# RWKV head pairs as two merged streams, with the dense products no longer tied behind their steps

## The chip, the cores and the metric

The kernel runs on one core of a Trainium2 chip. The metric is the device time of one execution in microseconds (us), the median of the runs shown.

## The reference

The reference is a block of two layers over 512 tokens of width 1024 in float32. Each layer is

```
x = x + 0.5 * swiglu(rms_norm(x, g_ffa), w_in_a, w_out_a)         # width 2816
h = rms_norm(x, g_mix);  z = h @ w_in                             # all branches' projections and the gates
ret  = retention(...)              # 8 heads, chunks of 128 tokens
dsa  = sparse_attention(...)       # 8 heads, top 128 keys by an index score
rwkv = rwkv7(...)                  # 8 heads of 64: token shift, low-rank decay, rate and gate, delta rule, group norm
x = x + sum over branches of sigmoid(gate_b) * (y_b @ p_b), through w_o
x = x + 0.5 * swiglu(rms_norm(x, g_ffb), w_in_b, w_out_b)
```

The RWKV part is a recurrence over the tokens: per head, a state of 64x64 is decayed, corrected by a rank-one term and read out at each token. The kernel computes it in chunks of 64 tokens. In a chunk the corrections depend on each other through a triangular matrix, which has to be inverted.

## The kernel before, in words

x is kept transposed (1024 features on 8 tiles of 128 partitions, 512 tokens). Every dense product runs in three passes on split operands (`mm3`, lines 109, 111, 113: high times high, high times low, low times high), so that one weight tile of 128 columns over 8 chunks is 24 products of 128x512. Weights come by DMA on SP's queue into four `raw` buffers (`load`, L54), are split by ScalarE and VectorE into three `whi` and three `wlo` buffers (`split`, L49 and L50), and each holds four chunks. TensorE writes to PSUM tiles `psd` (dense, 4 banks), `psr` (recurrence, 2) and `psf` (the rest, 2).

A mixer has three branches. `Ret` is retention by quarters, `Dsa` is the sparse attention, whose last part goes query tile by query tile and head pair by head pair: score products (`dot`, L710 and L711), a mask and softmax through VectorE, ScalarE and GpSimd (L805 to L810), turns of the weights L (L96), their split, and the products with v (L823, L824). Retention, attention, the 264-product gate blocks (`gates`) and the `merge` form one generator of dense work, `other()`. The third branch, `Rwkv`, goes by head pairs 0 to 3, and `pairs()` sets its order.

For a pair, `front` projects r, k and v (dense), `front2` makes decay, rate, the normalised key (turns of `bc`) and bonus, and the stacked operands `st` and `bk`. `mid` makes the chunk products z (L421, `psr<-stk,bk`), turns bk and v to token-major order, and inverts the triangles: their diagonal 32x32 blocks go to DRAM (`dn`) and back as `N`, one instance a partition (L457); GpSimd runs 31 steps on them (L466, L468); the inverse goes out as `dx` (L473) and back as `mt` (L479); 32 small products join the blocks (L487, L492). `chain` is the recurrence over 8 chunks, each of four dependent groups of products with copies by VectorE between (L504, L514, L524, L531, with the state `sv` made at L527). `post` is the group norm and the output: turns of Y (L96), scale and shift (L559), bonus (L561, GpSimd), gate product (L564) and its use (L565), then the result to DRAM, from where the merge reads it as `y` and splits it to `yh7` for pair 3.

The order of instructions on each engine is fixed when the kernel is built: a scheduler places instructions by the priority level in which they are traced ("rec" for the recurrence, then "split", "norm" for dense work, "late") with a simulated timeline, and an instruction may be tied behind another on its engine (`issue_after`). Before, the program ties dense work by hand. `K.fill(n, after)` (L78) traces n dense products of the queued work on TensorE behind a step of the pair, with counts from a table (lines 220 to 227):

```
FZ, FV, FD, FB, FE = 11, 38, 29, 5, 46
FP = 12, 11, 11, 15
FM = 6, 0, 2, 7
FC = 9, 7, 3, 5
```

An "urgent" queue gives the next pair's projections first place in it. Inside the inverse, after every fourth step, a pace product (L470, one column) waits for GpSimd's step, with dense products tied behind it, so that TensorE doesn't run ahead; there are 64 of them in the program. `pairs()` does, for each pair, the chain, then `next(p + 1)` (the next pair's `front2` and `mid`, tied behind the turns of v), then the `post`.

Of the kernel before, what the change touches and what calls it, by code (L numbers as in the profile page):

```python
# [7 lines left out]
P = 128  # L8
# [13 lines left out]
class Core:  # L22
    def __init__(self, tc, ctx):
        self.tc, self.nc, self.ctx = tc, tc.nc, ctx
        self.n = 0
        self.work, self.urgent, self.between = iter(()), deque(), True
        self.early = deque()
# [19 lines left out]
    def split(self, x, hi, lo):  # L47
        """exact parts of float32 for the one-pass products: x = hi + lo."""
# [8 lines left out]
    def wslot(self, src, n):  # L57
        """n <= 512 weight columns a partition, split."""
# [8 lines left out]
    def at(self, level):  # L67
        """what is traced here takes its place in that level of the scheduler's order."""
# [4 lines left out]
    def fill(self, n=None, after=None):  # L73
        """trace n products of the queued work, on the tensor engine behind `after`; n None: all that is urgent."""
        with ExitStack() as es:
            es.enter_context(self.at("norm"))
            if after:
                es.enter_context(self.tc.issue_after(after.ins))  # L78
            while n != 0 and (self.urgent or n):
                g = self.urgent[0] if self.urgent and self.between else self.work  # L80
                try:
                    new = next(g)
                except StopIteration:
                    if g is self.work:
                        break
                    self.urgent.popleft()
                    continue
                if g is self.work:
                    self.between = new
                if new == "wait":  # L90
                    break
                if n and not new:
                    n -= 1
# [11 lines left out]
    def mm3(self, out, a, b, start, stop):  # L105
        """three passes: hi*hi + hi*lo + lo*hi; a is stationary."""
# [9 lines left out]
    def dense(self, w, x):  # L116
        """w [128, K, 128] in DRAM, x: K split chunks of the transposed input -> PSUM [128 features, 512 tokens]."""
# [11 lines left out]
    def dense_tok(self, w, n, evac):  # L129
        """w [128, 8, n] in DRAM -> evac(token tile, PSUM [128 tokens, n features])."""  # L130
# [23 lines left out]
    def prep(self, x, c, gi, p):  # L154
        """chunk c of x^T -> split x*g, and its squares into the running sum."""
# [942 lines left out]
```

## Time and profile before

| | |
|---|---|
| median of 3 runs | 3111.48 us (3107.99 to 3112.62) |
| span of the profiled execution | 3103.6 us |
| around the span, against the median | 7.9 us |
| busy: TensorE, its weight loads | 2990.3 us, 2373.5 us |
| busy: VectorE, ScalarE, GpSimd | 1761.8, 1081.5, 715.2 us |
| products on TensorE | 14336 records |

The profiled execution is one of its own, not one of the three timed ones; the profile gives its span, and the table sets that against the median. TensorE is the bound, so the page is read by the time in which it is idle or runs at a lower clock: the windows give both by stretch, the list of waits tells for whom it waits, and the chain tells what lies behind the longest of these. A busy time counts a product's whole length although products are pipelined, so the spacing of starts, and not the mean length, tells what a product costs.

### The profile page before, as it was taken

To read this page: it belongs to the slowest core of one execution; us is meant where nothing else is said; L and a number is where in the kernel's file an instruction comes from. 1 tells how busy PE (TensorE), PEld (TensorE's weight loads), DVE (VectorE), ACT (ScalarE), POOL (GpSimd) and SP (SyncE) were. 2 spreads that over 40 slices of the span, in tenths; PEclk is the share of its full clock that TensorE was granted. 3 is DMA by queue.
4 is the path that set the end of the run, shared out by engine and by line. 5 is a ranking of instruction groups with operands and counts; after the bars stand their busy time and mean duration, and the time that the engine had idled before them with its cause. 6 is when DMAs were issued, how large, how long until landed. Compare 5 with 4: busy or idle time off the path is not lost.

```text
span 3103.6 us, 40717 instructions
## 1 busy us (share of the span) xinstructions
PE 2990.3 (96%) x14336; PEld 2373.5 (76%) x14336; DVE 1761.8 (57%) x3641; ACT 1081.5 (35%) x1892; POOL 715.2 (23%) x1186
## 2 busy tenths in 40 slices
PE   9999999999899999999999999999999899999998
PEld 7888877767667778888888888677776677788886
DVE  5443388758675675443344433887585746644433
ACT  4333343334333233333333333433333333333322
POOL 2110024342433031111011101243423340311100
PEclk9999999999899999999999999899999999999999
DMA  4223422223223452233322234222333135523232
GB/s 136 98 97 106 117 72 70 73 85 124 81 85 96 139 190 95 95 99 94 97 95 97 98 109 118 66 72 71 96 110 92 64 110 155 175 92 99 96 95 89
DMA packets 203580, 314.08 MB, mean 101 GB/s; under 512 B 46320, under 2 KB 60400, under 8 KB 203376
## 3 DMA queue, kind: packets, MB, share of 16 engines
q1 hardware_dynamic: 203376, 311.49, 32.2%
q8 instruction: 112, 1.84, 0.2%
q14 instruction: 92, 0.75, 0.1%
HBM read 277.86 MB, written 33.55 MB: 100 GB/s over the span
## 4 chain that ended last, share of the span: by engine, by line
PE 74%; DVE 10%; POOL 6%; DMA 6%; issue 3%; ACT 1%; SPq 0%; DVEq 0%; POOLq 0%; ACTq 0%
PE psd L113 22%; PE psd L109 22%; PE psd L111 22%; DMA N<-dn 3%; POOL cum L468 2%; POOL E L466 2%; DVE wlo L50 2%; PE psr L421 1%; DMA th<-th 1%; PE psr L504 1%; PE psf L96 1%; DMA dx<-cum 1%; DMA y<-y 1%; DVE cb L523 1%; PE psr L514 1%
## 5 line engine op out<-in xcount | busy, mean ns | idle before, releaser
L49 ACT ACTIVATE whi<-raw 128x512 fp32r<-128x512 f32 (+2 forms) x920 | 571.5, 622 | 1259.6 <-PE psd L111 927.2
L50 DVE TENSOR_TENSOR wlo<-raw,whi 128x512 fp32r<-128x512 f32 (+2 forms) x920 | 657.6, 715 | 560.0 <-ACT whi L49 543.9
L111 PE MATMUL psd<-xl,whi 128*128 128x512 f32 x2144 | 856.0, 399 | 2.4 <-DVE xl L161 2.4
L109 PE MATMUL psd<-xh,whi 128*128 128x512 f32 x2144 | 850.6, 397 | 1.5 <-DVE g L203 1.5
L113 PE MATMUL psd<-xh,wlo 128*128 128x512 f32 x2144 | 849.9, 396 | 0.1
L111 PEld LDWEIGHTS psd<-xl,whi 128*128 128x128 f32 x2144 | 406.7, 190 | 88.9 <-DVE xl L161 4.4
L109 PEld LDWEIGHTS psd<-xh,whi 128*128 128x128 f32 x2144 | 406.6, 190 | 88.5 <-issue 3.4
L113 PEld LDWEIGHTS psd<-xh,wlo 128*128 128x128 f32 x2144 | 406.9, 190 | 84.1 <-issue 1.4
L207 POOL TENSOR_TENSOR u<-s,u 128x512 f32<-128x512 f32 x88 | 141.2, 1605 | 841.0 <-DVE u L206 726.3
L109 PE MATMUL psd<-ah,whi 128*128 128x512 f32 x704 | 277.4, 394 | 0.0
L113 PE MATMUL psd<-ah,wlo 128*128 128x512 f32 x704 | 276.0, 392 | 0.0
L111 PE MATMUL psd<-al,whi 128*128 128x512 f32 x704 | 273.2, 388 | 0.0
L172 POOL TENSOR_TENSOR sq<-sq,sq 128x512 f32<-128x512 f32 x42 | 56.1, 1336 | 467.4 <-ACT sq L170 467.4
L113 PE MATMUL psd<-whi,xl 128*128 128x512 f32 (+1 forms) x384 | 160.6, 418 | 0.0
L111 PE MATMUL psd<-wlo,xh 128*128 128x512 f32 (+1 forms) x384 | 156.1, 407 | 0.0
L113 PEld LDWEIGHTS psd<-ah,wlo 128*128 128x128 f32 x704 | 132.1, 188 | 31.0
L109 PE MATMUL psd<-whi,xh 128*128 128x512 f32 (+1 forms) x384 | 155.1, 413 | 0.0
L111 PEld LDWEIGHTS psd<-al,whi 128*128 128x128 f32 x704 | 132.2, 188 | 29.6
L109 PEld LDWEIGHTS psd<-ah,whi 128*128 128x128 f32 x704 | 132.3, 188 | 26.3
L50 DVE TENSOR_TENSOR al<-u,ah 128x512 fp32r<-128x512 f32 x88 | 61.8, 702 | 153.6 <-ACT ah L49 153.4
L206 DVE TENSOR_TENSOR u<-psd,rb 128x512 f32<-128x512 f32 x88 | 60.9, 692 | 127.3 <-PE psd L113 127.3
L810 POOL TENSOR_SCALAR L<-L,mx 128x128 f32<-128x128 f32 (+3 forms) x64 | 71.4, 1118 | 199.4 <-DVE mx L809 99.0
(262 smaller groups left out, 3907.2 us busy)
## 6 DMA issues: line engine op xcount, KB each, us to landing
raw<-in_wf_dram SPq DMA_DIRECT2D x184, 256.0 KB
raw<-in_ffa_in_dram SPq DMA_DIRECT2D x176, 256.0 KB
raw<-in_ffb_in_dram SPq DMA_DIRECT2D x176, 256.0 KB
th<-th SPq DMA_DIRECT2D x96, 256.0 KB
raw<-in_ffa_out_dram SPq DMA_DIRECT2D x80, 256.0 KB
raw<-in_wt_dram SPq DMA_DIRECT2D x80, 256.0 KB
raw<-in_ffb_out_dram SPq DMA_DIRECT2D x80, 256.0 KB
x<-x SPq DMA_DIRECT2D x32, 256.0 KB
```

Of the source, the lines that this page charges most:

```text
L49: self.nc.scalar.activation(hi, x, AF.Copy)
L50: self.nc.vector.tensor_tensor(out=lo, in0=x, in1=hi.bitcast(F32), op=ALU.subtract)
L96: return self.nc.tensor.transpose(out, x, self.ident)
L109: nc.tensor.matmul(out, ah, bh, start=start, stop=False)
L111: nc.tensor.matmul(out, ah, bl, start=False, stop=False)
L113: nc.tensor.matmul(out, al, bh, start=False, stop=stop)
L172: nc.gpsimd.tensor_tensor(out=sq, in0=sq, in1=self.ssq[0], op=ALU.add)
L206: nc.vector.tensor_tensor(out=u, in0=pu, in1=self.rb, op=ALU.mult)
L207: nc.gpsimd.tensor_tensor(out=u, in0=s, in1=u, op=ALU.mult) # 2 * silu(g) * u
L466: nc.gpsimd.tensor_tensor(out=tv, in0=X[:, 0:n, u:u + 1].to_broadcast([P, n, w]), in1=N[:, u:u + 1, u + 1:].to_broadcast([P, n, w]), op=AL ...
L468: nc.gpsimd.tensor_tensor(out=X[:, 0:n, u + 1:], in0=X[:, 0:n, u + 1:], in1=tv, op=ALU.add)
L810: nc.gpsimd.tensor_scalar(out=x, in0=x, scalar1=mx[:, 3:4], scalar2=None, op0=ALU.mult)
```

## The change

It replaces the table and the ties by two generators. `ahead(d, p)` is a pair's `front2` and `mid`, `behind(d, p)` its `chain` and `post`. Each yields a number, an estimate of the time of the step just traced, and `pairs()` takes the stream whose sum is smaller; `behind` of a pair starts when `ahead` of it is done. Dense work is traced by `feed(n)` at level "norm", behind no step, and where it is traced has a fixed place once only: in `mid`, `FEED[p]` products (rounded up to whole blocks) and then the next pair's projections. The rest of the dense work follows in `K.feed()` after the last pair. The pace products and `next()` with its tie go. Buffers that two pairs can now need at once are doubled (`stk0`, `stk1`, `zb`, `bkt`, `sv0`, `sv1`, `gch`, `mt`); to pay for that, `N` lives in the one buffer of `bk`, retention's `m` in `S`'s, and attention's `sc` and `wk` in one tag of six. The y of `post` has a tile `yq` of its own. `dynamic_dma_scratch_size` is set to 1024. Line numbers fall by about 10 (109, 111, 113 become 99, 101, 103; L421 becomes L415, L487 L481, L504 L498, L564 L560).

```diff
-FZ, FV, FD, FB, FE = 11, 38, 29, 5, 46
-FP = 12, 11, 11, 15
-FM = 6, 0, 2, 7
-FC = 9, 7, 3, 5
+FEED = 100, 260, 260
...
-    def fill(self, n=None, after=None):
...
+    def feed(self, n=None):
+
+        with self.at("norm"):
+            while True:
                 try:
-                    new = next(g)
+                    new = next(self.work)
                 except StopIteration:
...
+                    return
+                if new == "wait" or n is not None and n <= 0 and new:
+                    return
+                if n is not None and not new:
                     n -= 1
...
     def pairs(self, blk):
...
+        d, t, n = [None] * 4, [0.0, 0.0], [0, 0]
+        g = [self.ahead(d, p) for p in range(4)], [self.behind(d, p) for p in range(4)]
+        while n[1] < 4:
+            e = 0 if n[0] < 4 and (n[1] == n[0] or t[0] <= t[1]) else 1
+            try:
+                with K.at("rec"):
+                    t[e] += next(g[e][n[e]])
+            except StopIteration:
+                n[e] += 1
+                if e == 0 and n[1] == n[0] - 1:
+                    t[1] = max(t)
         self.done = True
...
+    def ahead(self, d, p):
+        d[p] = yield from self.front2(p, *self.rkv)
+        yield from self.mid(d[p])
+
+    def behind(self, d, p):
+        yield from self.chain(d[p])
+        yield from self.post(d[p])
...
-                K.fill(FZ, zl)
+                yield 3
...
         if d["p"] < 3:
-            K.urgent.append(self.front(d["p"] + 1, self.blk))
-        K.fill(FV, self.gate)
-        # diagonal 32x32 blocks, one instance a partition
+            K.feed(FEED[d["p"]])
+            with K.at("norm"):
+                K.run(self.front(d["p"] + 1, self.blk))
+        yield 25
+
         dn = K.dram([4, 8, 32, 32], "dn", 2)
-        N = self.t("N", [P, 32, 32])
+        N = self.t("bk", [P, 8, P]).rearrange("p c t -> p (c t)").rearrange("p (s t) -> p s t", s=32)
...
-            if FI and (u % 4 == 3 or u == 30):
-                pace = nc.tensor.matmul(pz[0:1, u:u + 1], X[:, 0, u + 1:u + 2], K.ident[:, 0:1], start=True, stop=True)
-                K.fill(FI if u < 30 else FD, pace)
+            if u % 4 == 3 or u == 30:
+                yield 4 if u < 30 else 15
...
-            K.fill(FC[d["p"]], mm)
+            yield 2
```

How the change moves the work is seen in TensorE's order. The first place is the end of a mixer's dense work, in mixer 1. Before, these rows are around the first product that joins pair 3's blocks (L487; `psd<-xh` are gate products, `zb` its chunk products' tile):

```order
L111 MATMUL psd_9081<-xl_2874,whi_9111 128x512
L113 MATMUL psd_9081<-xh_2873,wlo_9112 128x512
L109 MATMUL psd_9081<-xh_2985,whi_9111 128x512
L111 MATMUL psd_9081<-xl_2986,whi_9111 128x512
L487 MATMUL psr_9229<-m_2068_9220,zb_8703 32x32 x8
L96 MATMUL psr_9320<-ident,Y_8236 64x128 x4
L823 MATMUL psf_6496<-X_6502,v_3127 128x256
L113 MATMUL psd_9081<-xh_2985,wlo_9112 128x512
L109 MATMUL psd_9141<-xh_2202,whi_9144 128x512
```

In the change, this is the last gate product (its third pass is L103 on `psd_9513`), with pair 2's chain (`psr_8078`, `psr_8116`), attention, and the first of pair 3's four groups of chunk products (L415) behind it:

```order
L101 MATMUL psd_9513<-xl_2986,whi_9534 128x512
L103 MATMUL psd_9513<-xh_2985,wlo_9535 128x512
L706 MATMUL psf_6253<-kh_3322,qs_6095 128x384
L707 MATMUL psf_6253<-kl_3323,qs_6095 128x384
L518 MATMUL psr_8078<-uv_1842_8097,bkt_7096 64x64
L518 MATMUL psr_8078<-uv_1843_8098,bkt_7096 64x64
L86 MATMUL psf_6263<-ident,L_6242 128x128
L498 MATMUL psr_8116<-sv_1640_7109,stk_1614_6984 128x64
L525 MATMUL psr_8078<-uv_1842_8097,zb_7019 64x64
L525 MATMUL psr_8078<-uv_1843_8098,zb_7019 64x64
L498 MATMUL psr_8116<-sv_1641_7110,stk_1615_6985 128x64
L415 MATMUL psr_8120<-stk_1838_8084,bk_8086 128x128 x4
```

and these are the rows around pair 3's first joining product (L481), 117 rows further:

```order
L706 MATMUL psf_6459<-kh_3322,qs_6295 128x512
L707 MATMUL psf_6459<-kl_3323,qs_6295 128x512
L706 MATMUL psf_6468<-kh_3322,qs_6298 128x512
L707 MATMUL psf_6468<-kl_3323,qs_6298 128x512
L481 MATMUL psr_8409<-m_1894_8400,zb_8119 32x32 x8
L498 MATMUL psr_8447<-sv_1864_8209,stk_1838_8084 128x64
L498 MATMUL psr_8447<-sv_1865_8210,stk_1839_8085 128x64
L486 MATMUL psr_8409<-mt_8399,m_1894_8400 32x32 x8
L481 MATMUL psr_8409<-m_1894_8400,zb_8119 32x32 x8
```

The joining product stood among gate products; it now stands among attention's scores (L706, L707) and the chain, and the first product of the merge (`psd<-yh`) comes 44 rows after it:

```order
L525 MATMUL psr_8495<-uv_1909_8500,zb_8119 64x64
L525 MATMUL psr_8495<-uv_1910_8501,zb_8119 64x64
L498 MATMUL psr_8519<-sv_1865_8210,stk_1839_8085 128x64
L99 MATMUL psd_9610<-yh_2135_9562,whi_9613 128x512
L99 MATMUL psd_9651<-yh_2135_9562,whi_9654 128x512
L508 MATMUL psr_8519<-cx_8522,mt_8399 64x64 x2
```

The second place is the end of pair 3 in mixer 1, the turns of Y, the gate product of `post` (L560) and the first product that reads its result (`psd_10170<-yh_2292`). In the change:

```order
L86 MATMUL psr_8654<-ident,Y_8446 64x128 x4
L86 MATMUL psr_8661<-ident,Y_8446 64x128 x4
L103 MATMUL psd_10228<-yh_2283_10146,wlo_10232 128x512
L99 MATMUL psd_10228<-yh_2286_10152,whi_10231 128x512
L101 MATMUL psd_10228<-yl_2287_10153,whi_10231 128x512
L103 MATMUL psd_10228<-yh_2286_10152,wlo_10232 128x512
L99 MATMUL psd_10228<-yh_2289_10158,whi_10231 128x512
L101 MATMUL psd_10228<-yl_2290_10159,whi_10231 128x512
L103 MATMUL psd_10228<-yh_2289_10158,wlo_10232 128x512
L560 MATMUL psr_8669<-sg_3592,g_703_3107 128x512
L99 MATMUL psd_10170<-yh_2292_10164,whi_10173 128x512
```

Between the turns and the reading product stand eight others. Before, 89 rows lie between L564 and the first reader of a rwkv block (`yh4`), and pair 3's comes after that; L564 itself stands among merge products:

```order
L109 MATMUL psd_10021<-yh_2235_9974,whi_10024 128x512
L111 MATMUL psd_10021<-yl_2236_9975,whi_10024 128x512
L564 MATMUL psr_9905<-sg_3592,g_703_3107 128x512
L113 MATMUL psd_10021<-yh_2235_9974,wlo_10025 128x512
L109 MATMUL psd_10021<-yh_2238_9980,whi_10024 128x512
```

## Rows read from the trace of the kernel before

**Rows 1.** The page, its first lines: the span, and TensorE's busy time, with the weight loads and the other engines behind it (share of the span, instructions).

```profile
span 3103.6 us, 40717 instructions
...
PE 2990.3 (96%) x14336; PEld 2373.5 (76%) x14336; DVE 1761.8 (57%) x3641; ACT 1081.5 (35%) x1892; POOL 715.2 (23%) x1186
```

**Rows 2.** The view of windows (us): first and last us, length, busy us of TensorE, of its weight loads, of VectorE, ScalarE and GpSimd (instructions in brackets), mean granted clock of TensorE, busy share of the DMA engines, GB/s. The first row is the merge of mixer 1, the second dense products alone, the last two the two mixers from their first pair to their last.

```profile
1100.00:1200.00 100.00, 95.60 (x420) 76.51 (x419) 60.52 (x87) 37.20 (x61) 32.17 (x22) 1.00 0.48 153
1200.00:1300.00 100.00, 100.00 (x445) 82.81 (x444) 49.95 (x76) 34.41 (x57) 15.46 (x10) 1.00 0.29 95
1946.00:2690.00 744.00, 696.03 (x3616) 525.74 (x3615) 519.89 (x1235) 263.60 (x493) 248.99 (x495) 0.95 0.32 99
406.00:1096.00 690.00, 647.58 (x3419) 488.16 (x3418) 482.58 (x1193) 249.36 (x468) 224.09 (x479) 0.95 0.30 93
```

**Rows 3.** The same view for four pieces of the first mixer in which the granted clock is 0.50 (433.7 to 447.4, 928.7 to 942.3, 785.3 to 799 and 1031.1 to 1041.3): the first of them, and the sum of the four.

```profile
433.70:447.40 13.70, 12.64 (x32) 8.45 (x33) 13.25 (x30) 2.26 (x5) 2.56 (x5) 0.50 0.09 29
...
sum 51.20, PE 42.65 PEld 30.50 DVE 40.13 ACT 8.85 POOL 5.58; mean PE 10.66 PEld 7.63 DVE 10.03 ACT 2.21 POOL 1.40
```

**Rows 4.** The list of waits of TensorE: what was waited for, us in total, times, longest.

```profile
PE psr L470 <- POOL cum L468: 25.4, 14, 4.9
PE psr L96 <- DVE bc L378: 19.7, 6, 4.4
PE psf L96 <- POOL L L810: 10.9, 10, 3.1
PE psr L421 <- DVE bk L403: 7.8, 6, 2.7
PE psf L824 <- DVE X L50: 6.5, 8, 1.9
```

**Rows 5.** The chain of waits in the first mixer, around pair 3's inverse: start us, us, what.

```profile
951.06 1.10 PE psr L421 x8
...
954.98 10.37 DMA N<-dn
965.49 0.46 POOL E L466
...
992.51 4.76 DMA dx<-cum
997.32 1.66 DMA mt<-dx
...
999.50 0.69 PE psr L487 x16
```

**Rows 6.** The same chain, around pair 0's inverse: three rows of the first mixer, then four of the second.

```profile
454.70 1.09 PE psr L421 x8
...
458.88 9.96 DMA N<-dn
...
509.09 0.62 PE psr L487 x16
...
1991.62 1.10 PE psr L421 x8
...
1995.77 4.15 DMA N<-dn
1999.92 7.80 issue
...
2048.91 0.62 PE psr L487 x16
```

**Rows 7.** The groups of instructions of TensorE by form, the line of the pace products: busy us, mean ns of one, idle time before them.

```profile
L470 PE MATMUL psr<-ident,cum 128*1 128x1 f32 x128 | 12.1, 164 | 25.8 <-POOL cum L468 25.4
```

**Rows 8.** The instructions of TensorE in order of time, around the end of the first mixer: start us, us, engine, line, operation. Two score products of the last query tile; the last gate product; two steps of pair 3's chain and the first merge product.

```profile
1007.02 0.40 PE L710 MATMUL psf<-kh,qs 128*128 128x512 f32 x1
...
1012.35 0.79 PE L710 MATMUL psf<-kh,qs 128*128 128x512 f32 x1
...
1026.01 0.39 PE L113 MATMUL psd<-xh,wlo 128*128 128x512 f32 x1
...
1031.28 0.69 PE L504 MATMUL psr<-sv,stk 128*128 128x64 f32 x2 [0.38 <-DVE sv L527]
...
1035.36 0.69 PE L504 MATMUL psr<-sv,stk 128*128 128x64 f32 x2 [0.37 <-DVE sv L527]
...
1036.84 1.20 PE L109 MATMUL psd<-yh,whi 128*128 128x512 f32 x2
```

**Rows 9.** The instructions of TensorE and ScalarE in order of time, at the end of the first mixer: the turns of pair 3's Y, and the split of its y for the merge.

```profile
1088.13 1.03 PE L96 MATMUL psr<-ident,Y 128*64 128x128 f32 x8
...
1102.92 0.63 ACT L49 ACTIVATE yh<-y 128x512 fp32r<-128x512 f32 x1 [0.92 <-DMA y<-y]
```

**Rows 10.** The groups of instructions of GpSimd in two stretches: pair 0's inverse (468 to 502 us), and the softmax line L810 in pair 3's (953 to 1000 us).

```profile
L468 POOL TENSOR_TENSOR cum<-cum,E 128x60 f32<-128x60 f32 (+24 forms) x31 | 11.9, 385 | 2.2
L466 POOL TENSOR_TENSOR E<-cum,N 128x60 f32<-128x60 f32 (+24 forms) x31 | 10.4, 336 | 7.9 <-DMA N<-dn 5.9
L598 POOL TENSOR_TENSOR m<-X,rss 128x128 f32<-128x128 f32 x8 | 3.5, 456 | 0.0
L603 POOL TENSOR_TENSOR kd<-X,kdec 128x128 f32<-128x128 f32 x4 | 2.0, 511 | 0.0
...
L810 POOL TENSOR_SCALAR L<-L,mx 128x512 f32<-128x512 f32 x3 | 4.7, 1568 | 5.5 <-DVE mx L809 5.5
```

More of the change, by code (lines that the diff above doesn't have):

```diff
@@ L25, in __init__ @@
         self.n = 0
-        self.work, self.urgent, self.between = iter(()), deque(), True
-        self.early = deque()
+        self.early, self.work = deque(), iter(())
         self.level = {"rec": 0, "split": 200000, "norm": 400000, "late": 800000}
@@ L71, in at @@
         self.level[level], self.tc.cur_priority = self.tc.cur_priority, s
-    def fill(self, n=None, after=None):
[L75 to L80, printed above, removed]
+    def feed(self, n=None):
+        with self.at("norm"):
+            while True:
                 try:
-                    new = next(g)
+                    new = next(self.work)
                 except StopIteration:
[L84 to L92, printed above, removed]
+                    return
+                if new == "wait" or n is not None and n <= 0 and new:
+                    return
+                if n is not None and not new:
                     n -= 1
@@ L314, in pairs @@
         K = self.K
-        K.run(self.lora(blk))
-        K.run(self.front(0, blk))
+        with K.at("norm"):
+            K.run(self.lora(blk))
+            K.run(self.front(0, blk))
         self.blk = blk
-        nxt = self.next(0)
-        for p in range(4):
-            d = nxt
-            K.fill(FM[p])
-            with K.at("rec"):
-                self.chain(d)
-            K.fill()
-            if p < 3:
-                nxt = self.next(p + 1)
-            with K.at("rec"):
-                self.post(d)
-        self.done = True
-    def next(self, p):
-        with self.K.at("rec"), ExitStack() as es:
-            if self.gate:
-                es.enter_context(self.tc.issue_after(self.gate.ins))
-            d = self.front2(p, *self.rkv)
-            self.mid(d)
-            return d
+        d, t, n = [None] * 4, [0.0, 0.0], [0, 0]
[9 more added lines that the diff above has]
+                    t[1] = max(t)
+        self.done = True
+    def ahead(self, d, p):
[4 more added lines that the diff above has]
+        yield from self.post(d[p])
     def front2(self, p, r, k, v):
@@ L447, in mid @@
         if d["p"] < 3:
[L448 to L449 removed]
+            K.feed(FEED[d["p"]])
+            with K.at("norm"):
+                K.run(self.front(d["p"] + 1, self.blk))
+        yield 25
         dn = K.dram([4, 8, 32, 32], "dn", 2)
[L452 removed]
+        N = self.t("bk", [P, 8, P]).rearrange("p c t -> p (c t)").rearrange("p (s t) -> p s t", s=32)
         for h in range(2):
@@ L531, in chain @@
                 nc.tensor.matmul(a[o, 192:256], zb[s, ck, o], uv[h][s], start=True, stop=True)
-            K.fill(FC[d["p"]] if ck < 7 else FE, mm)
+            yield 2
             for h in range(2):
@@ L940, in mixer @@
     K.work = other()
-    while next(K.work) != "index":
-        pass
+    with K.at("norm"):
+        while next(K.work) != "index":
+            pass
     rw.pairs(blk)
-    K.run(K.work)
+    K.feed()
     x = xnew()
```

40 lines of the change are left out of this document (23 added, 17 removed).

## The prediction

> **What bounds the kernel now.** I read the page first: TensorE is busy 2990.3 us of a span of 3103.6 us [rows 1]. So the most that better cover can give is small, and the question is where the last per cent is lost. The windows come next: outside the two mixers the engine is full (445 products of 128x512 in 100 us, 0.225 us each), while the mixer stretches have 690 us with 647.58 busy and 744 us with 696.03 busy, both at a mean granted clock of 0.95 [rows 2]. Two losses stand there. The first is idle time, 42.4 us in the first mixer and 48.0 in the second; 4.4 us of the same kind lie behind the first mixer, in its merge [rows 2], and the second window reaches to its merge too, so I count 43.6 for its pairs. The second is the clock: pieces of the mixer run at 0.50, TensorE's lower level of 1.2 GHz, and four such pieces together have 42.65 us of busy time in 51.20 us [rows 3]. At the full level that work would take half, so each microsecond at 0.50 costs 0.417 us. A mean of 0.95 is one tenth of the stretch at 0.50: 69 us and 74 us, which cost 28.7 and 31.0 us.
>
> The list of waits then says who is late: the pace products behind POOL's inverse (25.4 us), the turns of bc (19.7), the turns of the softmax tile L (10.9), the turned-block products behind bk (7.8), attention's products behind its split (6.5) [rows 4]. They are hops of the RWKV pair and of attention whose cover of dense products was too thin at that spot. Last comes the chain of waits, for the longest hop of all: in pair 3, from the last chunk product at 951.06 through a DRAM round trip of N (10.37 us), POOL's 31 steps and the way back through dx and mt to the first joining product at 999.50, 48.4 us [rows 5]. For pair 0 the same path is 54.4 us in the first mixer and 57.3 us in the second [rows 6]. Before, none of this time idles TensorE but for the pace products: it is full of dense products.
>
> **The change, part by part.** (1) The 64 pace products go. The trace has 128 records of them, 12.1 us of busy time [rows 7]; much of that runs beside its neighbours, so the bounds are 0 and 12.1; I take 8, near the recorded time, because each also breaks up a run of dense products.
>
> (2) The ties go, and the two streams are merged. In the order of the changed kernel the hops of front and chain have some 18 to 24 dense products before the next one, about 5 us at 0.225, in most of the mixer. A bare chain step takes 4.08 us at the lower clock (1031.28 to 1035.36) [rows 8], so these hops should be covered, and the waits behind bc, bk and L go with them. I take nearly all the idle time as saved, 42.4 and 43.6, but leave 4 us a mixer for hops that stay thin (bounds 0 and 10). The half-clock time goes with the idle time in front of it: 28.7 and 31.0 saved, with 8.5 a mixer returning for the pieces that new stalls start (bounds 4 and 16; one piece like that from 433.70 to 447.40, 13.7 us, costs 5.7) [rows 3]. (1) and (2) together save 8 + (42.4 - 4 + 28.7 - 8.5) + (43.6 - 4 + 31.0 - 8.5) = 8 + 58.6 + 62.1 = 128.7 us.
>
> (3) Pair 0's inverse loses cover. Between its last chunk product and the first joining product, the changed order has 41.6 us of TensorE's work in the first mixer and 39.2 in the second (estimates from the order, each form by its time from start to start in the trace of before). The path itself is 54.4 and 57.3 us [rows 6]. The stall is 12.8 and up to 18.1. N also shares a buffer with bk now, so its DMA waits for the turns of bk, some 8 us of work behind the last chunk product; that delays the path when those turns are late. I take 13 and 16, bounds 7 and 20.
>
> (4) The dense products run out too early. This is the largest term. The excerpts of the order show it: before, pair 3's first joining product stands among gate products; in the change, the last gate product stands 10 rows ahead of pair 3's first chunk products, and the first merge product comes 171 rows later. All of pair 3's inverse lies in between, with only pair 2's last steps and the last attention groups as cover. I put the work of those rows at 35 us in the first mixer and 38 in the second (by the same estimate: chain steps 11.5, attention 14, chunk products 3.6, turns 2.6, joining 2, the rest 1). The time it takes is the chain: up to the last chunk product two half-groups of attention, each 5.3 us from its score product to the next one (1007.02 to 1012.35), one chain step of 4.08 and 1.3 us of products, 16 in all [rows 8]; then the path of the inverse, 48.4 to 57.3, of which I take 51, near pair 3's own; then joining and about 3.8 chain steps before the merge starts, 15.5. That is 82.5 us, so 47 and 44 us are lost. Before, the same place cost little: the last gate product stands at 1026.01 and the first merge product at 1036.84, with attention and chain steps between [rows 8]. Bounds: 37 if attention and the inverse overlap better, 60 if POOL's queue is in the way.
>
> (5) Pair 3's result comes late for the merge. From its turns of Y at 1088.13 to the split of its y, at 1102.92 plus 0.63, before took 15.4 us, of which about 2.7 us is other work on the same engines [rows 9]. The changed order puts 3.3 us of TensorE's work between the turns and the first product that reads it (yh7), 1.7 in the second mixer. So 12.7 less that: 9.4 and 11.0, say 10 and 11; bounds 8 and 12.
>
> (6) The double buffers, the tiles that share a slot, and the smaller DMA scratch add no instruction on TensorE. I cost them at nothing: the chain streams they separate have slack where dense products stand, and if that cover is gone it is in (4) already. SP's weight loads stand in one queue with N, so N's wait for bk's turns holds back the loads behind it; the four raw and three split buffers ahead of TensorE hold 7 x 12 products of 0.225 us, some 19 us, more than the 8 us of that wait.
>
> Sum: lost 13 + 16 + 47 + 44 + 10 + 11 = 141; saved 128.7; net +12.3. The profiled span of 3103.6 lies 7.9 below the median 3111.48; the change is a difference within that span, so carried over: **3124 us**.
>
> A rule bears on N's leg. The trace gives 10.37 us for 512 KB in pair 3 [rows 5]. The Trainium skill's page DMA: Bandwidth & Descriptors, section Anatomy of one DMA, puts a transfer at a fixed 2.0 us plus bytes at 436 GB/s, given there for POOL's path; for 512 KB that would be 3.2 us, an estimate by that page, and with four uncovered inverses the sum would be 3095. The measured row decides, unless the leg is slow only because weight loads share the engines; that is rival A.
>
> **The rivals.** A, faster: N's leg is short once dense products, and with them the weight loads, thin out. For it speaks one row of 4.15 us in the second mixer [rows 6]; against it, that 7.80 us of issue follow, so POOL started no earlier, and the other row is 10.37 [rows 5]. At 4.15 each of the four uncovered inverses (two a mixer) is 6.2 us shorter: 25 us, giving 3099. If POOL's steps are also free of other work, another 4 us each, 3083. It decides once the path from last chunk product to join is below about 48 us in all four. The rule of the DMA page above would act in this way. Chance 0.27.
>
> B, much slower: the merge doesn't cover the hops, since the order is fixed ahead and each engine works strictly by it; where a real hop takes longer than the order allows, the waits behind bc, bk, L and the clock drops stay. Against it: 18 to 24 dense products a hop. If half of the saved idle and half-clock time stays, +60: 3184. Chance 0.06.
>
> C, slower: POOL works in order and has other work inside pair 0's and pair 3's steps. In pair 0 before, L598, L603 and L468 share the stretch, with 22.3 us of the inverse's own steps in 34 us; L810 with 1.57 us each stands in pair 3's [rows 10]. Ten L810 instead of three there are 11 us more for a path that nothing covers: +22 over both mixers, 3146. Chance 0.17.
>
> **How the numbers follow.** Forecast case 0.50 (3105 to 3142), A 0.27, B 0.06, C 0.17. A run of this kernel can tell about 0.2% from no change, 6.2 us. Faster by more: A, and 0.05 of the forecast's low end: 0.32. Within: 0.18, from the forecast's low half. Slower: the rest of the forecast's half (0.27), C and B: 0.50. The range, 3083 to 3160, reaches from A's second price over the forecast to beyond C, and leaves out B and little else. The forecast's own range is 3105 to 3142.
>
> **What would show it.** In the changed profile: no wait of pace products, and bc's and bk's waits under 8 us together; a stretch of 80 us in each mixer, around pair 3's inverse, with TensorE about half busy and no psd products; the inverse's first joining product waiting 12 us or more for mt in pair 0; yh7 waiting about 10 us. Wrong if the dense-free stretch is under 65 us, if N lands in 5 us, or if the waits behind bc and L810 remain at their size of before.

## The result, and the profile after

The changed kernel takes 3150.13 us (median of 4 runs, 3148.75 to 3152.47) against 3112.05 of the kernel before beside it: a ratio of 1.0124, 95% interval 1.011 to 1.0138. It is slower, on the side and in the range (3083 to 3160) that was forecast, but by more than three times the forecast's size, and beyond the forecast case's own 3105 to 3142: the span grows by 43.4 us, from 3103.6 to 3147.0, where +12.3 was worked out. All ratios here are of undisturbed executions; two of e11's six, its profiled one among them, were disturbed (4014.72 and 7333.44 us). The changed kernel's page answers to [rows 1]; the third row is the granted clock in 40 slices of the span.

```profile
span 3147.0 us, 40396 instructions
...
PE 3015.8 (96%) x14208; PEld 2408.6 (77%) x14208; DVE 1755.4 (56%) x3641; ACT 1080.3 (34%) x1892; POOL 717.9 (23%) x1186
...
PEclk9999998889996799999999999979999958999999
```

TensorE has 128 records fewer and is busy 25.5 us longer. The clock is behind that: the mean is 0.948 for 0.975 before, so the time at 1.2 GHz (twice what the mean lacks to 1, times the span) rose from 155 us to 327 us. The view of windows, with the columns of [rows 2], shows where: the two mixers in wide windows, then three stretches.

```profile
400.00:1200.00 800.00, 741.35 (x3661) 568.51 (x3661) 531.20 (x1257) 277.55 (x515) 257.89 (x507) 0.89 0.32 97
1946.00:2750.00 804.00, 749.53 (x3787) 580.33 (x3787) 543.82 (x1293) 287.03 (x533) 262.03 (x523) 0.91 0.33 101
...
571.00:640.00 69.00, 65.96 (x291) 50.98 (x292) 42.18 (x102) 17.57 (x29) 13.60 (x28) 0.73 0.17 53
966.50:1061.00 94.50, 70.89 (x354) 50.16 (x353) 51.33 (x165) 23.24 (x50) 37.15 (x90) 0.56 0.11 32
2514.00:2610.00 96.00, 71.61 (x347) 50.31 (x347) 50.81 (x165) 21.80 (x49) 37.91 (x89) 0.55 0.09 22
```

The same two wide windows of the kernel before:

```profile
400.00:1200.00 800.00, 753.17 (x3881) 572.88 (x3881) 549.21 (x1288) 291.06 (x536) 262.75 (x516) 0.96 0.32 101
1946.00:2750.00 804.00, 756.03 (x3889) 575.45 (x3888) 551.78 (x1291) 289.29 (x535) 258.34 (x502) 0.95 0.33 101
```

Idle time, length less busy, grew only from 46.8 to 58.6 us and from 48.0 to 54.5. The list of waits of TensorE (us in total, times, longest) tells that it is other idle time:

```profile
PE psf L86 <- POOL L L806: 28.8, 12, 6.1
PE psf L615 <- ACT L L755: 16.2, 2, 8.2
PE psd L99 <- ACT yh L48: 14.2, 2, 7.3
PE psd L103 <- DVE wlo L49: 6.3, 4, 3.5
...
PE psr L384 <- DVE bc L376: 2.0, 1, 2.0
```

The waits of the pace products are gone, and those behind bc fell from 19.7 us to 2.0 [rows 4]: the merge does cover the short hops. In their place stand waits behind the softmax (L806) and two new ones of some 8 us a mixer, behind L755 and behind pair 3's y.

The largest place is the forecast one. TensorE in order of time, with idle time in brackets: the last gate product; pair 3's last chunk products; two turns of L; the first joining product; the first merge product; and, 94 us on, the first product that reads pair 3's y.

```profile
966.32 0.39 PE L103 MATMUL psd<-xh,wlo 128*128 128x512 f32 x1
...
983.62 1.70 PE L415 MATMUL psr<-stk,bk 64*128 64x128 f32 x7
...
1011.49 0.47 PE L86 MATMUL psf<-ident,L 128*128 128x128 f32 x1 [4.52 <-POOL L L806]
...
1026.47 0.47 PE L86 MATMUL psf<-ident,L 128*128 128x128 f32 x1 [3.31 <-POOL L L806]
...
1040.36 1.05 PE L481 MATMUL psr<-m,zb 32*32 32x32 f32 x16 [2.71 <-DVE mx L803]
...
1060.89 1.20 PE L99 MATMUL psd<-yh,whi 128*128 128x512 f32 x2
...
1154.90 1.65 PE L99 MATMUL psd<-yh,whi 128*128 128x512 f32 x3 [6.84 <-ACT yh L48]
```

From the last gate product to the merge are 94.6 us (101.0 in the second mixer), with no dense product in it. The inverse inside it, on TensorE, SP's queue and GpSimd: the last turn of bk, the read of N, which is now in bk's buffer, GpSimd's first step and its last.

```profile
991.19 1.11 PE L86 MATMUL psr<-ident,bk 128*128 128x128 f32 x4
...
992.34 0.55 SPq L453 DMA_DIRECT2D bk<-dn  x1
...
1002.15 0.24 POOL L461 TENSOR_TENSOR E<-cum,bk 128x31 f32<-128x31 f32 x1 [6.68 <-DMA bk<-dn]
...
1033.12 0.21 POOL L463 TENSOR_TENSOR cum<-cum,E 128x8 f32<-128x8 f32 x1
```

Against [rows 5], leg by leg for pair 3 of the first mixer (us; the last chunk product starts at 951.9 and at 984.9):

| leg | before | after |
|---|---|---|
| last chunk product to the issue of N | 3.1 | 7.4 |
| N, issue to GpSimd's first step | 10.5 | 9.8 |
| GpSimd's 31 steps | 27.0 | 31.2 |
| dx, mt, first joining product | 7.0 | 7.0 |
| sum | 47.6 | 55.4 |

N waits longer, for the turns of bk, whose buffer it shares: it is issued as the last turn ends. GpSimd has four scalings of L (L806) between its steps for two before (L810), and the bonus of pair 2's y (L557). Its groups, from first to last step, two rows of the changed kernel and one of the kernel before:

```profile
L806 POOL TENSOR_SCALAR L<-L,mx 128x512 f32<-128x512 f32 x4 | 6.3, 1566 | 0.2
...
L557 POOL TENSOR_TENSOR yq<-yq,bv 128x512 f32<-128x512 f32 x1 | 1.3, 1281 | 0.0
...
L810 POOL TENSOR_SCALAR L<-L,mx 128x512 f32<-128x512 f32 x2 | 3.1, 1568 | 0.0
```

The new wait of pair 0 stands at another place than the join. One row each of GpSimd, VectorE, ScalarE and TensorE in order of time:

```profile
493.39 0.29 POOL L762 TENSOR_SCALAR_AFFINE_SELECT X<-X 128x128 f32<-128x128 f32 x1
...
493.72 0.56 DVE L767 MAX8 m<-X 128x8 f32<-128x384 f32 x1 [7.51 <-POOL X L762]
...
495.42 0.60 ACT L755 ACTIVATE L<-psf 128x512 f32<-128x512 f32 x1 [8.30 <-DVE X L758]
...
496.16 1.55 PE L615 MATMUL psf<-X,kd 128*64 128x128 f32 x12 [7.97 <-ACT L L755]
```

A causal select of 0.29 us stands in GpSimd's queue among the inverse's steps; VectorE's top-key search waits for it, ScalarE's copy out of a `psf` bank for VectorE, and TensorE for the bank. The read of N, dx, mt and the join are not in this chain; of the inverse, only GpSimd's steps are, as what stands ahead in the queue.

### The profile page after: what moved, and what is told of

It is laid out like the page before. It is cut to its first block, busy times and chain, and to the rows that moved or that the text cites. A ratio compares the mean times of both kernels' runs of the same rounds, so it can differ in the third digit from the quotient of the medians.

```text
span 3147.0 us, 40396 instructions
## 1 busy us (share of the span) xinstructions
PE 3015.8 (96%) x14208; PEld 2408.6 (77%) x14208; DVE 1755.4 (56%) x3641; ACT 1080.3 (34%) x1892; POOL 717.9 (23%) x1186
## 5 line engine op out<-in xcount | busy, mean ns | idle before, releaser
L103 PE MATMUL psd<-xh,wlo 128*128 128x512 f32 x2144 | 846.6, 395 | 5.8 <-DVE wlo L49 5.8
L103 PEld LDWEIGHTS psd<-xh,wlo 128*128 128x128 f32 x2144 | 405.2, 189 | 91.8 <-DVE wlo L49 7.6
L103 PE MATMUL psd<-ah,wlo 128*128 128x512 f32 x704 | 276.0, 392 | 0.0
L103 PEld LDWEIGHTS psd<-ah,wlo 128*128 128x128 f32 x704 | 132.1, 188 | 31.0
L101 PEld LDWEIGHTS psd<-al,whi 128*128 128x128 f32 x704 | 132.2, 188 | 29.6
L103 PE MATMUL psd<-whi,xl 128*128 128x512 f32 (+1 forms) x384 | 151.5, 395 | 0.0
L99 PE MATMUL psd<-whi,xh 128*128 128x512 f32 (+1 forms) x384 | 140.3, 400 | 0.0
L99 PE MATMUL psd<-yh,whi 128*128 128x512 f32 x256 | 102.4, 410 | 14.2 <-ACT yh L48 14.2
```

The lines of the kernel that those rows point to most:

```text
L99: nc.tensor.matmul(out, ah, bh, start=start, stop=False)
L101: nc.tensor.matmul(out, ah, bl, start=False, stop=False)
L103: nc.tensor.matmul(out, al, bh, start=False, stop=stop)
```

## The experiments

All stand on the changed kernel but for e7 and e10. Each time has the kernel before beside it on the same chip: 3110.14 us for e1 to e4, 3107.22 for e5 to e8, 3107.33 for e9 and e10, 3109.93 for e11 and e12. "Loss" below is worked out per mixer: for each product the time from its start to the next one's, less what its form takes so in the trace of before (the estimate behind the prediction's 35 and 38 us), split into idle time, what is extra at the half clock, and what is extra at the full clock. Over the two wide windows it gives 107.0 and 109.2 us before and 144.6 and 121.2 after; the difference of 49.6 less 7.6 us for the work of the pace products is 42.0 of the 43.4.

**e1_hold: dense work kept back for pair 3.**

```diff
+F2, FC, FZ, FV = 150, {2: 5}, {3: 8}, {3: 1000}
+    def tie(self, n, ins):
+        with self.at("norm"), self.tc.issue_after(ins.ins):
...
+        if d["p"] == 2:
+            K.feed(F2)
+        if d["p"] in FV:
+            K.tie(FV[d["p"]], self.gate)
...
+                K.tie(FZ.get(d["p"], 0), zl)
...
+            K.tie(FC.get(d["p"], 0), mm)
```

`tie` traces n products of the queued work behind an instruction. 150 gate products come behind pair 2's front, 5 behind each of the three hops of pair 2's chain steps, 8 behind each of pair 3's groups of chunk products, and the rest behind pair 3's turn of v.

> The changed kernel with part of its gate products held back from pair 2 on: 5 tied behind each hop of pair 2's chain, 8 behind each group of pair 3's chunk products, all the rest behind pair 3's turn of v; 150 are traced right behind the last front. Nothing is added or left out. Theory A (the loss is the stretch without dense products around pair 3's inverse, 94.5 us long in mixer 1 with 35 us of work at full clock): it shrinks to under 25 us, and 35 to 50 us a mixer come back, 3150 -> 3050 to 3080. Theory B (the loss comes from the merged streams themselves, in their hops and small products, wherever the dense products stand): less than 20 us in all, 3130 to 3150, with the clock at 0.5 as long as before.

Measured 3151.55 us, ratio 1.0136 [1.0117, 1.0155]: nothing gained, and theory A failed. The stretch between the gate products and the merge shrank to 28.9 and 29.6 us, as intended, but a new one opened in pair 2's inverse, and in mixer 2 the clock now falls among retention's products, where the changed kernel has 1.00 (the window rows):

```profile
850.00:910.00 60.00, 42.92 (x208) 29.45 (x207) 29.26 (x87) 16.89 (x37) 35.82 (x85) 0.63 0.15 41
...
2130.00:2200.00 70.00, 66.03 (x292) 51.23 (x293) 42.78 (x102) 17.92 (x30) 13.47 (x28) 0.73 0.18 54
```

From 821 to 911 us 35.5 us are lost. The bare stretch was moved, not removed: the amount of dense work is fixed, and two inverses want it. The gain expected of filling pair 3's did not come in the total.

**e2_warm: other products in the end stretch.** Products of 128x512 whose results aren't used, three for each bank of the last query tile's attention and two for each bank of the chains of pairs 2 and 3. They add work.

```diff
+            for _ in range(2 if d["p"] > 1 else 0):
+                nc.tensor.matmul(a, K.xg[0][0][:, :P], K.xg[0][0], start=True, stop=True)
...
+    def warm(self, ps, qt):
+        for _ in range(3 if qt == 3 else 0):
+            self.nc.tensor.matmul(ps, self.K.xg[0][0][:, :P], self.K.xg[0][0], start=True, stop=True)
```

> The changed kernel with products of 128x512 that nothing reads, added in the stretch without dense products: three into each bank of the last query tile's attention and two into each bank of the chain of pairs 2 and 3, overwritten at once by the real products (about 16 us of added work a mixer at full clock). Theory C (the stretch is long because TensorE works at 1.2 GHz in it, 70.9 of its 94.5 us busy): granted clock near 1.0 there, its length 94.5 -> 75 to 80, the total 3150 -> 3110 to 3125 although work is added. Theory D (it is long because pair 3's inverse is waited for, 55 us from its last chunk product to its first joining product, whatever the clock): clock near 1.0, length 88 to 100, the total 3140 to 3165.

Measured 3167.04 us, ratio 1.0188 [1.0166, 1.0209]. The stretch in three windows: to the last chunk product, the inverse's path, and from the first joining product to the merge.

```profile
967.60:987.60 20.00, 17.68 (x88) 13.74 (x87) 13.46 (x34) 4.11 (x9) 2.55 (x5) 0.66 0.16 47
987.60:1041.90 54.30, 34.55 (x171) 22.87 (x169) 26.08 (x87) 12.46 (x27) 30.57 (x77) 0.84 0.09 23
1041.90:1075.80 33.90, 30.52 (x170) 21.65 (x170) 12.55 (x46) 6.11 (x14) 4.51 (x8) 0.55 0.10 30
```

In the changed kernel these were 18.6, 55.5 and 20.5 us at 0.64, 0.56 and 0.50. Theory C failed; D is right on the path, though the stretch of 108.2 us and the time lie above its ranges. The clock of the path rose to 0.84, and the path stayed: it is set by the DMA legs and GpSimd, not by TensorE's clock. The end, at 0.55, is 13.4 us longer, with added products in its chain. So the end stretch won't go with a better clock alone; that the tail would shorten with a better clock isn't shown, since its clock didn't rise.

**e3_mask: the causal select off GpSimd's queue.**

```diff
-                nc.gpsimd.affine_select(out=dgl, in_=dgl, pattern=[[-1, P]], compare_op=ALU.is_ge, fill=-1e30, base=0,
-                                        channel_multiplier=1)
+                nc.vector.tensor_tensor(out=dgl, in0=dgl, in1=c["tri"], op=ALU.add)
```

> The changed kernel with the causal mask of the index scores added by VectorE (one tensor_tensor on 128x128) in place of GpSimd's affine select. Theory E (pair 0's stall of 8 us a mixer is a queue on GpSimd: the select stands behind the inverse's steps, VectorE waits for it, ScalarE for VectorE, and TensorE for the bank that ScalarE empties): the wait of L615 for L755 goes from 16.2 us to under 4, and since the order then has shorter runs of retention products (7 us of work in place of 10 to 15 in mixer 1), the clock stays up more of the time between 571 and 640 us: 3150 -> 3110 to 3130. Theory F (pair 0's stall is the inverse's path and only shows at this place): a stall of about the same size turns up at the first joining product L481, the total 3145 to 3155.

Measured 3136.96 us, ratio 1.0086 [1.0067, 1.0106], 11 us less over the kernel before than the changed kernel (26.8 for 38.1). The time lies between the ranges of theories E and F. The wait behind L755 is gone; the first joining product (L481) now waits 10.7 us in all, 3.6 and 4.0 of them at pair 0 in the two mixers, which is F's way; and, as E has it, the stretch from 571 to 640 us, with two of retention's runs, has no half clock left:

```profile
571.00:640.00 69.00, 69.00 (x395) 54.48 (x393) 48.43 (x122) 23.06 (x41) 20.76 (x35) 1.00 0.29 86
```

The loss of mixer 1 from 571 to 641 us fell from 18.8 to 1.7. The end stretch is no shorter (101.0 and 102.0 us for 94.6 and 101.0).

**e4_both: e1 and e3 together.**

> The edits of e1_hold and e3_mask together. If A and E both hold, their gains add: 3150 -> 3020 to 3060, below the kernel before (3112). If B and F hold: 3120 to 3150.

Measured 3115.37 us (10 runs), ratio 1.002 [1.001, 1.003]: the best of the merged orders, and still behind the kernel before. Each against the kernel before beside it, the two edits are worth 33 us together, and 11 (e3) and none (e1) alone. One reason is in the rows: where e1's order let the clock fall in mixer 2, e4 has it at 1.00, as it has from 571 to 640 us.

```profile
2130.00:2200.00 70.00, 70.00 (x420) 55.11 (x419) 39.98 (x97) 25.50 (x46) 28.98 (x75) 1.00 0.28 81
```

Losses 108.2 and 125.6; the end stretch 24.6 and 44.7 us. The time lies between the two ranges expected.

**e5_counts and e6_counts_mask: no feeds, the dense work by counts behind the pairs' hops, as in the kernel before, but with the streams still merged; e6 with e3's edit as well.**

```diff
-FEED = 100, 260, 260
+FEED = 0, 0, 0
+F2, FC, FZ, FV = 0, {0: 12, 1: 11, 2: 8, 3: 4}, {0: 8}, {0: 180, 3: 120}
```

> The changed kernel with merged streams, double buffers and all, but every dense product of a mixer's rest tied by count as the kernel before did: 12, 11, 8 and 4 behind each hop of the chain of pairs 0 to 3, 8 behind each group of pair 0's chunk products, 180 behind pair 0's turn of v and 120 behind pair 3's; FEED is gone. Theory G (the fixed order spends dense products where nothing waits: 73 to 78 us of work stand between the last chunk product and the first joining product of pairs 1 and 2, where the path takes some 50 to 55, and they are missing at pair 3): pair 3's stretch without dense products is gone and no other takes its place, idle plus half-clock loss in the mixers falls from about 235 us to 130 or less, 3150 -> 3050 to 3100. Theory H (two streams on two psr banks and one GpSimd get in each other's way wherever the dense products stand): 3110 to 3145.

> e5_counts with the mask of e3_mask added by VectorE. Theory G: 10 to 20 us below e5_counts, 3035 to 3085. Theory H: 3100 to 3135.

Measured 3129.44 us, ratio 1.0073 [1.0052, 1.0094], and 3139.37, 1.0098 [1.008, 1.0117]. Theory G failed, and e3's edit gains nothing here. In e5 no bare stretch is longer than the 25 us ahead of the merge, and the mean clock is 0.97, near that of before, yet the losses are 126.2 and 123.2. The list of waits shows what took their place:

```profile
PE psd L120 <- DVE wlo L49: 31.4, 20, 4.9
PE psf L103 <- POOL L L830: 21.9, 10, 3.6
PE psd L116 <- ACT yh L48: 10.7, 3, 5.2
```

The dense products are now there, but their weight splits are late on VectorE, which the two streams share with them.

**e7_before_mask: e3's edit in the kernel before.**

> The kernel before with only the mask of e3_mask. If the 13 us of e3_mask are the mask's own, 3090 to 3100; if they come from GpSimd's queue only where the changed order lets its inverse steps block the select, 3105 to 3113.

Measured 3112.55 us (10 runs), ratio 1.0014 [1.0001, 1.0028]. The select costs nothing in the old order, so e3's gain belongs to the changed one.

**e8_warm_ret: two unused 128x512 products for each bank of retention, 144 in all (some 32 us at 0.225).**

```diff
+    def warm(self, ps):
+        for _ in range(2):
+            self.nc.tensor.matmul(ps, self.K.xg[0][0][:, :P], self.K.xg[0][0], start=True, stop=True)
...
         pk = K.ps()
+        self.warm(pk)
```

> The changed kernel with two products of 128x512 that nothing reads in front of the real ones in each of retention's nine banks of a quarter (144 in all, about 32 us of work at full clock). Theory K (a run of small products alone drops the clock, with TensorE busy all the while): the clock between 570 and 650 us goes from 0.73 to 0.95 or more; the total 3140 to 3165. Theory L (only idle time drops the clock): it stays near 0.73 there, the total 3175 to 3185.

Measured 3170.2 us, ratio 1.0198 [1.0174, 1.0223], 25 us more over the kernel before than the changed kernel, for 32 us of added work. The window of retention:

```profile
519.00:693.00 174.00, 169.80 (x948) 133.09 (x947) 121.24 (x314) 57.25 (x98) 68.50 (x150) 1.00 0.23 70
```

and the same window of the changed kernel:

```profile
519.00:693.00 174.00, 169.44 (x876) 132.16 (x876) 120.46 (x301) 57.50 (x96) 65.94 (x141) 0.89 0.21 65
```

TensorE is busy for the same 169 us in both; the clock is 1.00 with the added products and 0.89 without. But the idle time has moved: e8's lies at the end of the window, from 687.6 us on, while the changed kernel has 2.04 us right ahead of the drop at 572 us and 1.68 us right ahead of that at 620. From 571 to 640 us e8 has none (the first row below), so e8 doesn't part theory K from theory L. Other rows do. The second is the later piece of the changed kernel, where TensorE works without a break and the clock stays at 0.50; the last two are of the kernel before, whose clock fell for 3.4 us after 51 us without any idle time.

```profile
571.00:640.00 69.00, 69.00 (x383) 54.42 (x382) 49.49 (x128) 21.25 (x36) 19.03 (x36) 1.00 0.21 63
...
620.00:640.00 20.00, 20.00 (x76) 15.59 (x75) 8.92 (x23) 4.96 (x8) 2.56 (x7) 0.50 0.07 14
...
560.00:611.20 51.20, 51.20 (x304) 39.23 (x303) 34.13 (x84) 17.90 (x31) 15.98 (x29) 1.00 0.22 74
611.20:614.60 3.40, 3.40 (x9) 2.64 (x9) 3.26 (x6) 1.08 (x2) 2.68 (x3) 0.50 0.00 0
```

So a drop needs no idle time ahead of it, and L is out. Whether the short idle times helped at 572 and 620 us isn't shown.

**e9_tuned: e4 with other counts** (`F2, FC, FZ, FV = 190, {2: 3, 3: 2}, {3: 8}, {3: 138}`).

> The changed kernel with POOL's causal select replaced as in e3, and the dense work held back as in e4, with other numbers: 190 gate products behind pair 2's front, 3 behind each hop of pair 2's chain, 8 behind each of pair 3's groups of chunk products, 138 behind pair 3's turn of v and 2 behind each hop of pair 3's chain. By the fixed order, the work between the last chunk product and the first joining product is 40, 75, 43 and 52 us in mixer 1's pairs 0 to 3 (e4: less in two pairs). Theory M (what is left of the loss is bare inverse paths of some 55 us, each short of cover by its missing work): 25 to 40 us under e4, 3075 to 3095. Theory N (once the long bare stretches are filled, the loss comes back as many short waits for VectorE's weight splits and the softmax, as in e5): 3110 to 3140, with waits on wlo over 20 us in sum.

Measured 3127.3 us, ratio 1.006 [1.0044, 1.0076]: theory M failed. The end stretch is down to 6.8 and 7.2 us, yet pair 2's inverse from 850 to 910 us loses 32.3 us (29.6 in e4). Theory N's range holds, not its sign: waits on `wlo` are 14.2 us, not over 20.

**e10_before_no_pace: the kernel before without its pace products.**

```diff
-                pace = nc.tensor.matmul(pz[0:1, u:u + 1], X[:, 0, u + 1:u + 2], K.ident[:, 0:1], start=True, stop=True)
-                K.fill(FI if u < 30 else FD, pace)
+                K.fill(FI if u < 30 else FD, self.gate)
```

> The kernel before without its 64 pace products; the dense products that stood behind each are tied behind the turn of v instead. Step 1 of the prediction (the pace products cost 8 us of TensorE's time, bounds 0 and 12.1, and their wait of 25.4 us moves to the first joining product): 3098 to 3108, L487 waiting some 20 us more. Rival P (the waits at the pace products are a cost of the pace itself: without them TensorE has other work there and the 25.4 us are gained too): 3075 to 3090. Rival Q (pace keeps the order good: without it the dense work in the inverse runs out early and the joins stand bare): 3115 or more.

Measured 3125.08 us, ratio 1.0057 [1.0044, 1.007]: rival Q. The edit takes away two things together, the pace and the spread of the dense products that stood behind it. What is extra at the full clock fell from 31.9 to 24.0 and from 32.2 to 24.2, but idle time rose by 8.1 and 6.0 and the half-clock loss by 11.9 and 11.3. The first joining product (here L486) waits instead:

```profile
PE psr L486 <- DVE m L479: 19.6, 7, 3.8
```

**e11_softmax_off_pool and e12_both_softmax: the softmax's scaling on ScalarE, in the changed kernel and in e4.**

```diff
-                    nc.gpsimd.tensor_scalar(out=x, in0=x, scalar1=mx[:, 3:4], scalar2=None, op0=ALU.mult)
+                    nc.scalar.activation(x, x, AF.Copy, scale=mx[:, 3:4])
```

> The changed kernel with one line moved to another engine: the softmax's last scaling (L806, 1.57 us each on POOL, four of them between the steps of pair 3's inverse in each mixer) on ScalarE. Theory Q (POOL's in-order queue is part of the size of the end stretch: the scalings lengthen the inverse, and the softmax behind the inverse's steps is what TensorE idles for): the path from the last chunk product to the join falls from 55.5 us to 48 to 50 in pair 3, the waits behind L from 28.8 us to under 12, the end stretch to 82 to 88 us; 3115 to 3138. Theory R (the stretch is set by the inverse's path and by a half clock that stays as long as no dense product runs; what TensorE waits for inside it is of no account): the waits move to the first joining product, the stretch shortens by less than 6 us; 3138 to 3150.

> e4 (causal select off POOL, gate products held back for pair 3) with the softmax's scaling on ScalarE as well. Theory Q: POOL's queue is also part of the waits behind L of 14.6 us there and of the inverse paths of pairs 2 and 3 (66 us each); 3095 to 3110, level with the kernel before or under it. Theory R: nothing of it sets the end; 3112 to 3120, as e4.

Ratios 1.0119 [1.0097, 1.0141] and 1.003 [1.0018, 1.0042] (3119.7 us): theory R by the time, both times; e11's rows aren't read. In e12 GpSimd's 31 steps of pair 3 take 24.8 and 25.0 us for 29.2 and 25.9 in e4, so the scalings do lengthen them, but the time doesn't follow: the waits behind L fell from 14.6 us to 6.3, and others grew.

```profile
PE psd L115 <- DVE wlo L49: 24.3, 14, 4.9
PE psr L499 <- DVE m L492: 21.6, 3, 9.7
...
PE psf L98 <- ACT L L826: 6.3, 6, 1.6
```

## Why the prediction was right in sign and range, and too small

| us, mixer 1 / mixer 2 | forecast | measured |
|---|---|---|
| (4) end stretch: length | 82.5 / 82.5 | 94.6 / 101.0 |
| (4) its work at full clock (estimate) | 35 / 38 | 35.4 / 38.0 |
| (4) lost | 47 / 44 | 59.2 / 63.0 |
| (3) pair 0's inverse, lost | 13 / 16 | 21.4 / 23.1 |
| (2) half-clock loss left outside these | 8.5 / 8.5 | 24.8 / 6.5 |
| (2) idle time left outside these, merge included | 8.4 / 8.4 | 17.0 / 10.0 |
| (5) wait for pair 3's y | 10 / 11 | 6.8 / 7.3 |
| extra at full clock, change | not in the sum | -14.8 / -19.2 |

The rows on losses and idle time, measured less forecast, add up to 30.3 of the 31.1 us by which the growth of 43.4 passes 12.3. That the time stayed inside the range is in part luck: without the 34.0 us of the last row, which no term held, it would be 3184 us.

**Step 4 was the right mechanism with too small a size, and it is the step that failed most.** Its work is the same estimate of the same rows, so that it agrees is no test; the time put on it was too short. The forecast took 16 us ahead of the last chunk product, 51 for the path and 15.5 behind; 18.6, 55.5 and 20.5 were measured in mixer 1, and 23.2, 55.6 and 22.2 in mixer 2. The path was taken near pair 3's old one, but the price of N's shared buffer was put on pair 0 alone (4.3 us here, by the table of legs), and GpSimd's added scalings and bonus (4.2 us) stood in rival C only. The tail is some four chain steps of 4.08 us [rows 8] and joins, with attention's products among them at the half clock.

**Step 2 was right on the hops and wrong on the clock.** The waits of pace and bc went as forecast. The forecast let the half-clock time go with the idle time in front of it; that link doesn't hold, and the kernel before already had a drop without any (611.2 us). From 571 to 640 us TensorE is idle for 3.04 us of 69 and its clock is 0.73, and e8 gives 1.00 there with 128x512 products in retention's runs. By the fixed order, and the same estimate of each form's time, retention's runs without dense products have 14.9, 10.1, 14.6 and 6.2 us of work in mixer 1, for 7.0, 6.2, 7.6 and 6.0 before. This costs 18.8 us, which no term held. In mixer 2 the runs behind the first are shorter (6.4, 9.7 and 5.9 us) and from 2095 to 2250 us only 2.6 us go to the half clock; in e3, with 6.9, 7.1 and 6.6, mixer 1 passes the place at 1.00. The length of a run doesn't tell alone: mixer 2's 9.7 us, without idle time, pass at 1.00, and mixer 1's 10.1 us, with 2.89 us of idle time in them, don't. Of idle time, 4 us a mixer and the merge's own 4.4 were to be left; 17.0 and 10.0 were, in many short waits.

**Step 3 had about the right idle time by the wrong way.** 11.2 and 11.9 us are idle from pair 0's last chunk product to the end of its join and what follows (to 524 and 2095 us), for 13 and 16. But the join isn't what waits: TensorE waits for the select in GpSimd's queue, by the four rows above and e3. The half clock behind it adds 9.6 and 11.0. When e3 took the select away, the idle time of the place fell by only 2.5 us in mixer 1 (11.2 to 8.7) and its loss by 0.2: the forecast stall for mt stood right behind (L481, 3.6 us here).

**Step 5** was 3 to 4 us too large; why wasn't looked into.

**Step 1** was sized well by the removed work (7.6 us by spacing, 8 forecast) and missed what the pace did for the order. e10 shows both sides: without the pace, 16 us less is lost at the full clock, and the kernel still gets 0.57% slower. Those products were a brake that spread the dense work over the inverse, and 25.4 us of waiting [rows 4] was its price, not a loss to be won.

**The rivals.** A is out: N took 9.8 us with a DMA share of 0.11 in the stretch, and 9.7 to 11.1 in the eight inverses of the changed kernel, and none of the four uncovered paths is under 55 us. The Trainium skill's page DMA: Bandwidth & Descriptors, section Anatomy of one DMA, gives figures for GpSimd's path from which 3.2 us follow (an estimate by that page); no measured leg of N, which is on SP's queue, agrees. B is out on the hops, though clock drops did stay. C's price, 3146 us, came nearest, and C was right that GpSimd's queue counts, in pair 0 and in the end stretch, but not in its way: pair 0's 31 steps took 30.2 us in both mixers, less than before (32.9 and 33.1), and with the scalings off GpSimd (e11) the time is the same.

**The signs** that the prediction named came out mixed. The pace and bc waits and the dense-free stretch were as forecast, and N did not land in 5 us. But no joining product of pair 0 waits 12 us, and the waits behind L did not shrink: they grew from 10.9 us to 28.8. Waits behind bc and L that remain were a sign of being wrong, and the half on L came.

**What stays open** is whether a merged order can beat the hand-tied one. Filling each bare stretch (e1, e4, e9) opens another in pair 2's inverse; spreading by counts (e5) has none over 25 us, and loses as much in short waits on VectorE's splits; e12 shows such waits change place when one is taken away. Which queue sets the limit then was not settled. That N's shared buffer costs what the table says was read from the trace and not tried.

## What to carry to other kernels

Before ties are taken out of a full engine's order, count for each long round trip how much filling work the new order leaves it, and how long the engine would stand with small products only: the time of such a stretch must be taken from the chain and from rows at the lower clock, not from its work. A wait in the list can be a brake that spreads scarce work; before it is booked as a gain, look at what runs out later. On an engine that works in order, look for short instructions of another branch behind a long chain, and follow who waits for them.

## What the runs showed of the hardware

- The granted clock was 0.73 over 69 us in which TensorE was busy for 65.96 us, in two pieces with hardly a dense product (572 to 589 and 620 to 640 us), where products of retention and attention follow each other; it was 1.00 over the same stretch with some 128x512 products in it (e8), and in e3, whose runs without dense products are shorter, both without idle time there. In the kernel before it fell to 0.50 at 611.2 us though TensorE had not been idle since 560 us.
- The 512 KB read of N from DRAM took 9.8 us from issue to use with the DMA engines at a share of 0.11, much as the 10.51 us before, where the share was 0.30 over the mixer [rows 2, 5].
- A 0.29 us instruction behind GpSimd's chain held TensorE for 7.97 us, through two other engines and a PSUM bank; with it moved to VectorE (e3), the idle time of the place fell from 11.2 us to 8.7 only.
